# A transformer block on one Trainium2 core: twelve forget-gate sets are computed as three double blocks with the tokens standing

## The chip, the core and the metric

The kernel runs on one core of one Trainium2 chip. Its work is spread over the core's engines: TensorE multiplies matrices (PE in the profile; PEld is the loading of the operand that stands in the array), VectorE (DVE) and ScalarE (ACT) do elementwise work, GpSimd (POOL) does small work and issues DMAs, and SyncE (SP) issues DMAs alone. Each engine runs its instructions strictly in the order in which they were written for it, and waits at each one until its operands are there. The metric is the device time of one execution in microseconds (us); the kernel before takes 1574.6 us, the median of three runs.

## The reference, cut to what matters

The reference computes one block of a hybrid network on 256 tokens `x` and 256 context tokens `ctx`, all in float32. Both are normalised and modulated, and then projected by one wide matrix `w_in`, whose columns are cut into queries, keys, values, gates, forget gates and so on:

```
xn = rmsnorm(h, norm_gain[l]) * (1.0 + scale) + shift
cn = rmsnorm(hc, norm_gain[l]) * (1.0 + scale_c) + shift_c
aq, ak, av, ag, hq, hff, hfb, hi, hg, ma, mb = split_columns(xn @ w_in[l])
...
f = lbf + (1.0 - lbf) * jax.nn.sigmoid(z.astype(jnp.float32))
return to_heads(jnp.log(f)), to_heads(1.0 - f)
```

The change touches `hff` and `hfb`, the forget gates forward and backward. Each has 16 heads of 128 columns, and both are needed for the 256 tokens of `x` and the 256 of `ctx`. After the projection each value goes through a sigmoid and a scale and offset that belong to its column. The later scan over the tokens works with one column in one partition, tokens along the row. Besides the forget gates, the values `hi` and the attention's keys and values are needed for all 512 tokens too.

## The kernel before

**How a product is made.** Weights come from device memory in chunks of 128x1024 numbers by SP (`wload`, L66; five buffers, tag `raw`). ScalarE makes the high part `wh` of a chunk, VectorE the rest `wl` (`two`, L635 and L636; three buffers each). TensorE then multiplies high by high and low of the tokens, and low by high, so float32 is kept to the needed accuracy. The tokens are kept as `xHL`, high and low, with the model dimension on the partitions.

**Two ways to a product of all 512 tokens.** Both use the same scheme of seven products in place of eight, in which token halves, halves of the model dimension and column halves are combined beforehand. In each the steps 0 to 6 (`ORDER`) take weights b11, t1, t2, b22, t3, b21, t4, where the t are differences of weight chunks that VectorE makes (`combos` L616, `less` L693), and sums of tokens S stand ready in `S`.

- `quad_col(d, h0)` makes one *set*: two heads (256 columns) of the direction d, columns on the partitions. The weights stand in the array and the tokens move: per step eight matmuls of 512 columns (L660) and eight of 256 (L663, low weights by high tokens only). Its four weight loads fetch rows of 512 bytes. The results are joined by VectorE (L653, L654), go through sigmoid and scale (L682, L683), and are stored to `F_dr` by ScalarE's DMA queue.
- `quad_wide(co, dsts)` makes one *double block*: 1024 columns, tokens on the partitions. Tokens stand and weights move, so every matmul has 512 columns (L754 with high weights, L758 with low). It runs in two halves s of the model dimension; each half has seven steps of two chunks c, twelve matmuls to a chunk. Loads fetch rows of 2048 bytes. Results are taken from PSUM by ScalarE (L735, L744) and VectorE (L739) and are stored by GpSimd's queue (L726), in the second half with an adding DMA.

**Order of the work.** In this stage the order of TensorE is as written; the order on the other engines is set by a scheduler from priorities, and splits of chunks have a high one. The stage runs: three output gates, three double blocks with `quad_wide` (`hi` twice, then attention keys and values), thirteen sets with `quad_col` (of the sixteen sets, three were made at the start of the program). Then come the eight pairs of heads, which load the forget gates from `F_dr`.

**Buffers that matter here.** Tag `sm` has three tiles of 128x512 in the pool `base`. Each DMA on the two hardware queues (SP, ScalarE) takes one of eight semaphores in turn, which is seen below as DMAHW0 to DMAHW7; a DMA waits until the one that had its semaphore before has landed. DMASW are those of GpSimd's queue. `behind_chunk()` places what is issued under it behind the latest split on ScalarE and VectorE.

Of the kernel before, what the change touches and what calls it, by code (L numbers as in the profile page):

```python
# [7 lines left out]
F32 = mybir.dt.float32  # L8
F32R = mybir.dt.float32r
U8 = mybir.dt.uint8  # L10
AF = mybir.ActivationFunctionType
ALU = mybir.AluOpType
PSUM = bass.MemoryType.PSUM

P = 128
# [3 lines left out]
HD = 128  # L19
# [5 lines left out]
C_HQ, C_FF, C_FB, C_HI, C_HG = 5120, 7168, 9216, 11264, 13312  # L25
# [13 lines left out]
def block_kernel(ctx: ExitStack, tc: tile.TileContext, x, c, cx, c_ctx, w_ada, b_ada, norm_gain, w_in,  # L39
                 b_merge, lb_f, lb_b, hg_gain, w_oh, sink, w_oa, w_out, fin_gain, cst, msk, out):  # L40
    nc = tc.nc
    pe, act, dve, pool = nc.tensor, nc.scalar, nc.vector, nc.gpsimd

    def pl(name, bufs=1, **kw):
        return tc.tile_pool(name=name, bufs=bufs, **kw)
# [5 lines left out]
    base = ctx.enter_context(pl("base"))  # L51
# [3 lines left out]
    dram = ctx.enter_context(pl("dram", space=bass.MemoryType.DRAM))  # L55
# [13 lines left out]
    last_hi, last_lo = [None], [None]  # L69

    def behind_chunk():

        both = ExitStack()
        both.enter_context(tc.issue_after(last_hi[0]))
        both.enter_context(tc.issue_after(last_lo[0]))
        return both
# [103 lines left out]
    lbc = pad.tile([P, 4, 16], F32, name="lbc")  # L180
# [45 lines left out]
    few.tile([P, 16], F32, name="space1")  # L226
    gate_rows = dram.tile([KT, P], F32, name="gate_rows")
    F_dr = [[dram.tile([P, 1024], F32, name=f"F{d}_{n}") for n in range(8)] for d in range(2)]
    v_dr = [[dram.tile([P, 1024], F32, name=f"v{g}_{t}") for t in range(2)] for g in range(4)]
    hg_dr = [dram.tile([P, 1024], F32, name=f"hg{g}") for g in range(4)]  # L230
    ma_dr = [dram.tile([P, 1024], F32, name=f"ma{n}") for n in range(4)]
# [286 lines left out]
    def run(g):  # L518
        for _ in g:
            pass  # L520
# [40 lines left out]
    with pl("sp", reuse_waits="tile") as sp:  # L561
# [8 lines left out]
        def token_sums(g):  # L570

            def a(h, kh):
                return [X[:, 8 * kh + 4 * g: 8 * kh + 4 * g + 4, :].rearrange("p k (a h t) -> p k a h t", a=2, h=2)
                        [:, :, :, h, :].bitcast(F32) for X in (xH, xL)]

            def v(t):
                return t.rearrange("p (k a t) -> p k a t", k=4, a=2)

            def put(i, t):
                ks = slice(4 * g, 4 * g + 4)  # L580
                dst = [S[:, z, i, ks, :].rearrange("p k t -> p (k t)") for z in range(2)]
                act.activation(dst[0], t, AF.Copy)
                dve.tensor_tensor(dst[1], t, dst[0].bitcast(F32), op=ALU.subtract)

            def step(out, x_, y_, op):
                dve.tensor_tensor(out, x_, y_, op=op)

            a11, a12, a21, a22 = a(0, 0), a(0, 1), a(1, 0), a(1, 1)
            p, q = tmp(), tmp()
            step(v(p), a21[0], a22[0], ALU.add)  # L590
            step(v(q), a21[1], a22[1], ALU.add)
            step(p, p, q, ALU.add)
            put(0, p)
            step(v(q), v(p), a11[0], ALU.subtract)
            step(v(q), v(q), a11[1], ALU.subtract)
            put(1, q)
            for i, b in ((3, a12), (2, a22)):
                step(v(p), b[0], v(q), ALU.subtract)
                step(v(p), v(p), b[1], ALU.add)
                put(i, p)  # L600
# [30 lines left out]
        def two(src):  # L631
            h = wp.tile([P, 1024], F32R, tag="wh", name="wh", bufs=3)
            lo = wp.tile([P, 1024], F32R, tag="wl", name="wl", bufs=3)
            with tc.high_priority(PRIO):
                act.activation(h, src, AF.Copy)  # L635
                dve.tensor_tensor(lo, src, h.bitcast(F32), op=ALU.subtract)  # L636
            return h, lo

        def quad_col(d, h0):

# [43 lines left out]
                               bias=lbc[:, d, h0 + i: h0 + i + 1])  # L684
            nc.scalar.dma_start(F_dr[d][h0 // 2], F.rearrange("p i t -> p (i t)"))

        def quad_wide(co, dsts):


            def less(o, x_, y_):  # L690
                with tc.high_priority(PRIO):
                    for o_, a_, b_ in zip(o, x_, y_):
                        dve.tensor_tensor(o_, a_, b_, op=ALU.subtract)  # L693

            def weights(s):

                def load(n):
                    return [wload(w_in, 1024 * (n[0] == "2") + 512 * s + 256 * c, 2,
                                  (co + 512 * (n[1] == "2"),), 512)[0] for c in range(2)]

                u = [tmp(), tmp()]
                b11 = load("11")
                yield b11
                b12 = load("12")
                less(u, b12, b11)
                yield u
                b22 = load("22")
                less(u, b22, u)
                yield u
                yield b22  # L710
                less(b12, b22, b12)
                yield b12
                b21 = load("21")
                yield b21
                less(u, b21, u)
                yield u

            for s in range(2):
                m_ = [[bank8(), bank8()] for _ in range(3)]
                into = {0: (0, True), 1: (1, True), 2: (0, False), 3: (1, False), 4: (0, False), 5: (2, True),  # L720
                        6: (0, False)}
                kept = {}

                def store(o, t, c, z=slice(0, 2)):
                    kw = {"accum_op": ALU.add} if s else {}
                    nc.gpsimd.dma_start(dsts[c][t].rearrange("p (z c) -> p z c", z=2)[:, z, :], o, **kw)  # L726

                def done_with(i, m):

                    with tc.high_priority(2 * PRIO):  # L730
                        if i < 3:
                            kept[i] = fp.tile([P, 2, 512], F32, tag="F1" if i == 2 else "F0", name="part",
                                              bufs=1 if i == 2 else 2)
                            for z in range(2):
                                act.activation(kept[i][:, z, :], m[z], AF.Copy)  # L735
                        elif i < 6:
                            o = kept[5 - i]
                            for z in range(2):
                                dve.tensor_tensor(o[:, z, :], m[z], o[:, z, :], op=ALU.add)  # L739
                            store(o, *((0, 1), (1, 1), (0, 0))[i - 3])  # L740
                        else:
                            for z in range(2):
                                o = base.tile([P, 512], F32, tag="bb", name="part", bufs=2)
                                act.activation(o, m[z], AF.Copy)  # L744
                                store(o, 1, 0, z)

                for (i, _, st_), tiles in zip(ORDER, weights(s)):
                    z_, fresh = into[i]
                    for c in range(2):
                        h, lo = [a.rearrange("p (k c) -> p k c", k=2) for a in two(tiles[c])]  # L750
                        jz = [(j, z) for j in range(2) for z in range(2)]
                        for j, z in jz:
                            for a in range(2):
                                pe.matmul(m_[z_][z], st_(4 * s + 2 * c + j)[:, a, z, :], h[:, j, :],  # L754
                                          start=fresh and c == 0 and j == 0 and a == 0, stop=False,
                                          skip_group_check=True)
                        for j, z in jz:
                            pe.matmul(m_[z_][z], st_(4 * s + 2 * c + j)[:, 0, z, :], lo[:, j, :], start=False,  # L758
                                      stop=c == 1 and j == 1, skip_group_check=True)
                    done_with(i, m_[z_])  # L760

        with tc.manual_schedule(engines={mybir.EngineType.PE}):
            for g in range(3):
                run(output_gate(g))
                send()
                if g < 2:
                    token_sums(g)
            for co, dsts in ((C_HI, v_dr[:2]), (C_HI + 1024, v_dr[2:]), (C_K, kv_dr)):
                quad_wide(co, dsts)
            for n in range(1, 8):  # L770
                for d in range(2):
                    if (d, n) != (0, 1):
                        quad_col(d, 2 * n)

    def bias_row(row, n, late=None):
        bb = base.tile([P, 512], F32, tag="bb", name="bb", bufs=2)
# [631 lines left out]
    fg = [at.tile([P, 1024], F32, tag="v", name="fg"), None]  # L1408
# [58 lines left out]
    for i in range(4):  # L1467
        src = w_out[4 * i * P: 4 * (i + 1) * P, D - 256:].rearrange("(k p) c -> p k c", p=P)
# [7 lines left out]
    for n in range(3):  # L1476
        bo = [bank() for _ in range(2)]
        for k0 in range(0, KT, 2):
            h, lo = wchunk(w_out, k0 * P, 2, n * 512, 512)
# [8 lines left out]
    for k0 in range(0, KT, 4):  # L1488
        h, lo = wchunk(w_out, k0 * P, 4, D - 512, 256)
# [85 lines left out]
```

## Time and profile before

| what | value |
|---|---|
| runs of the kernel before | 1571.52, 1574.95, 1574.6 us; median 1574.6 us |
| profiled execution: its time, its span | 1575.11 us, 1573.3 us |
| TensorE busy | 1550.6 us of the span, 9946 matmuls |
| three double blocks | 198.36 to 426.84 us of the span |
| thirteen sets | 426.84 to 686.40 us of the span |

The profile is of one execution. A row of groups reads: line, engine, operation, output<-inputs, shape, count, then busy time, mean duration of one in ns, and the idle time of the engine just before with what ended it. A row of a stretch (windows) gives its length and, for each engine, busy us and count, then TensorE's granted clock, the share of DMA time and GB/s. A row of the timeline gives start, length, engine, line and operation, how many instructions it merges, and in brackets the idle time before it. TensorE's durations overlap (a matmul of 512 columns is shown with 389 ns, while the next begins 227 ns after it), so a pace is read from starts, not from durations.

### The profile page before, as it was taken

How to read it: one execution, taken by the hardware profiler on the slowest of the kernel's cores; microseconds unless marked ns; L12 is line 12 of the kernel's file. 1: busy time of each engine (PE TensorE's matmuls, PEld its weight loads, DVE VectorE, ACT ScalarE, POOL GpSimd, SP SyncE). 2: the span in 40 equal slices, each digit the busy share in tenths (PEclk: the TensorE clock that was granted, in tenths of full speed). 3: DMA queues.
4: the chain of work that ended last, by engine and by line, in shares of the span. 5: the costliest groups of instructions: out<-in, count | busy, mean ns of one | idle time of the engine just before them, and what ended most of it. 6: DMA issues, size and time to landing. Idle time of an engine off the chain costs nothing.

```text
span 1573.3 us, 25961 instructions
## 1 busy us (share of the span) xinstructions
PE 1550.6 (99%) x9946; PEld 1292.0 (82%) x9946; DVE 1198.4 (76%) x1758; ACT 879.5 (56%) x1380; POOL 158.4 (10%) x298
## 2 busy tenths in 40 slices
PE   7999999999999999999999999999999999999998
PEld 4558888888888888888888888888888888888887
DVE  4448987777788877879888897887977777757764
ACT  4326545454555555665566666565665767744442
POOL 2000000110100000011212221121121000000000
PEclk9999999999999999999999999999999999999999
DMA  9996645656644444477677887877777844458651
GB/s 368 386 387 237 215 156 159 180 160 183 153 121 134 135 134 134 141 266 246 235 247 239 289 276 244 282 236 242 244 256 243 281 153 157 161 186 289 226 195 68
DMA packets 232812, 339.99 MB, mean 216 GB/s; under 512 B 12368, under 2 KB 137712, under 8 KB 231920
## 3 DMA queue, kind: packets, MB, share of 16 engines
q1 hardware_dynamic: 201808, 249.54, 48.0%
q0 software_dynamic: 21376, 70.38, 14.4%
q10 hardware_dynamic: 9504, 18.42, 3.2%
q8 instruction: 78, 1.28, 0.3%
q14 instruction: 46, 0.38, 0.1%
HBM read 300.53 MB, written 37.76 MB: 215 GB/s over the span
## 4 chain that ended last, share of the span: by engine, by line
PE 89%; DMA 4%; DVE 4%; issue 2%; ACT 1%; POOL 0%; SPq 0%; POOLq 0%; DVEq 0%; ACTq 0%
PE pj L100 12%; PE pj L101 12%; PE pj L103 12%; PE pj L154 7%; PE pj L754 5%; PE pm L754 4%; PE pj L157 4%; PE pm L660 3%; PE pj L660 3%; PE pj L758 3%; DMA raw<-in_w_in_dram 2%; PE pm L758 2%; PE pa L323 2%; PE pj L427 2%; PE pj L663 2%
## 5 line engine op out<-in xcount | busy, mean ns | idle before, releaser
L85 ACT ACTIVATE wh<-raw 128x1024 fp32r<-128x1024 f32 x284 | 298.7, 1058 | 231.1 <-PE pj L101 150.6
L86 DVE TENSOR_TENSOR wl<-raw,wh 128x1024 fp32r<-128x1024 f32 x284 | 344.1, 1220 | 92.1 <-ACT wh L85 91.3
L100 PE MATMUL pj<-wh,xHL 128*128 128x512 f32 (+1 forms) x768 | 298.6, 390 | 1.1 <-ACT wh L85 1.1
L101 PE MATMUL pj<-wh,xHL 128*128 128x512 f32 (+1 forms) x768 | 294.8, 385 | 0.0
L103 PE MATMUL pj<-wl,xHL 128*128 128x512 f32 (+1 forms) x768 | 202.7, 385 | 0.0
L100 PEld LDWEIGHTS pj<-wh,xHL 128*128 128x128 f32 x768 | 144.4, 188 | 29.6 <-ACT wh L85 1.3
L101 PEld LDWEIGHTS pj<-wh,xHL 128*128 128x128 f32 x768 | 144.5, 188 | 27.6
L103 PEld LDWEIGHTS pj<-wl,xHL 128*128 128x128 f32 x768 | 142.0, 188 | 28.8
L635 ACT ACTIVATE wh<-raw 128x1024 fp32r<-128x1024 f32 x100 | 105.8, 1058 | 94.0 <-PE pj L754 37.4
L635 ACT ACTIVATE wh<-T 128x1024 fp32r<-128x1024 f32 x75 | 79.6, 1062 | 109.2 <-DVE T L616 23.4
L636 DVE TENSOR_TENSOR wl<-raw,wh 128x1024 fp32r<-128x1024 f32 x100 | 121.6, 1220 | 21.9 <-ACT wh L635 21.8
L154 PE MATMUL pj<-xHL,wh 128*128 128x512 f32 x512 | 130.3, 396 | 0.3 <-ACT wh L85 0.3
L154 PEld LDWEIGHTS pj<-xHL,wh 128*128 128x128 f32 x512 | 92.4, 189 | 17.3 <-ACT wh L85 0.5
L636 DVE TENSOR_TENSOR wl<-T,wh 128x1024 fp32r<-128x1024 f32 x75 | 91.5, 1219 | 13.6 <-ACT wh L635 13.5
L157 PEld LDWEIGHTS pj<-xHL,wl 128*128 128x128 f32 x512 | 69.8, 190 | 5.1
L204 DVE SCALAR_TENSOR_TENSOR acc<-hgw,cg,acc 128x512 f32<-128x512 f32 x60 | 44.8, 747 | 35.1 <-DMA hgw<-in_w_ada_dram 35.1
L157 PE MATMUL pj<-xHL,wl 128*128 128x256 f32 x512 | 71.3, 282 | 0.0
L928 DVE TENSOR_TENSOR A<-A,X 128x512 f32<-128x512 f32 x96 | 61.6, 683 | 0.1
L541 POOL DMA_DIRECT2D hgw<-in_w_ada_dram x64 | 35.1, 548 | 235.2 <-DVE acc L204 148.0
L754 PE MATMUL pj<-wh,S 128*128 128x512 f32 x224 | 55.3, 389 | 0.0
L660 PE MATMUL pm<-S,wh 128*128 128x512 f32 x208 | 52.5, 394 | 1.6 <-ACT s L667 1.6
L660 PE MATMUL pj<-S,wh 128*128 128x512 f32 x208 | 52.5, 394 | 0.1
(346 smaller groups left out, 2847.5 us busy)
## 6 DMA issues: line engine op xcount, KB each, us to landing
raw<-in_w_in_dram SPq DMA_DIRECT2D x300, 512.0 KB, 4.7
raw<-in_w_ada_dram SPq DMA_DIRECT2D x64, 512.0 KB, 8.0
hgw<-in_w_ada_dram POOLq DMA_DIRECT2D x64, 256.0 KB, 4.6
raw<-in_w_o_hgrn_dram SPq DMA_DIRECT2D x32, 512.0 KB, 3.7
raw<-in_w_o_attn_dram SPq DMA_DIRECT2D x32, 512.0 KB, 4.1
raw<-in_w_out_dram SPq DMA_DIRECT2D x28, 512.0 KB, 4.1
F<-F POOLq DMA_DIRECT2D x16, 512.0 KB, 6.7
F<-F ACTq DMA_DIRECT2D x13, 512.0 KB, 4.3
```

What stands on the lines that cost most here:

```text
L85: last_hi[0] = act.activation(h[:, :n], raw[:, :n], AF.Copy).ins
L86: last_lo[0] = dve.tensor_tensor(lo[:, :n], raw[:, :n], h[:, :n].bitcast(F32), op=ALU.subtract).ins
L100: pe.matmul(o, s[0], m[0], start=first, stop=False)
L101: pe.matmul(o, s[1], m[0], start=False, stop=False)
L103: pe.matmul(o, s[0], m[1], start=False, stop=last)
L154: pe.matmul(o.rearrange("p (a t) -> p a t", a=2), h[:, j, cs_], xHL[:, :, k0 + j, :T], start=k0 + j == 0, stop=False)
L157: pe.matmul(o[:, :T], lo[:, j, cs_], xH[:, k0 + j, :T], start=False, stop=k0 + j == KT - 1)
L635: act.activation(h, src, AF.Copy)
L636: dve.tensor_tensor(lo, src, h.bitcast(F32), op=ALU.subtract)
L660: pe.matmul(m_[z].rearrange("p (z a t) -> p z a t", z=2, a=2), h[:, k, :], mv(k), start=fresh and k == 0, stop=False, skip_group_check=True)
L754: pe.matmul(m_[z_][z], st_(4 * s + 2 * c + j)[:, a, z, :], h[:, j, :], start=fresh and c == 0 and j == 0 and a == 0, stop=False, skip_grou ...
L758: pe.matmul(m_[z_][z], st_(4 * s + 2 * c + j)[:, 0, z, :], lo[:, j, :], start=False, stop=c == 1 and j == 1, skip_group_check=True)
```

## The change

Of the thirteen sets twelve are no longer made by `quad_col`; the set of the backward heads 2 and 3 stays there and comes last. The 24 heads of the twelve sets (3072 columns) are made by three further calls of `quad_wide`, ahead of the other three. For that `quad_wide` takes two column starts instead of one with a fixed distance.

Since `quad_wide` leaves tokens on the partitions and the scan wants columns there, each half of 512 columns is stored to a new tensor `f_dr` of 512 tokens by 512 columns in device memory. A new generator `forget_rows` handles one head: four DMAs on SP's queue load the head's 512x128 numbers as squares of 32x32 (runs of 128 bytes) into one tile `blk`, then VectorE turns each square in one instruction into the tile `fg`, ScalarE applies sigmoid, scale and offset, and its queue stores the result to `F_dr` as before. `blk` and `fg` are both tiles of tag `sm`. `rows_on` is called ahead of a chunk's split in the double blocks (all but the first six chunks of each), and moves the head in hand one step: in the first step the DMAs, then two that do nothing, and in the next the rest, together with the first step of the following head. So a head takes three chunks. `two` now records its splits, so that `behind_chunk()` works there.

```diff
+    f_dr = [dram.tile([512, 512], F32, name=f"f{j}") for j in range(6)]
...
-                act.activation(h, src, AF.Copy)
-                dve.tensor_tensor(lo, src, h.bitcast(F32), op=ALU.subtract)
+                last_hi[0] = act.activation(h, src, AF.Copy).ins
+                last_lo[0] = dve.tensor_tensor(lo, src, h.bitcast(F32), op=ALU.subtract).ins
             return h, lo
+
+        def forget_rows(d, h, src):
+
+
+            blk = base.tile([P, 512], F32, tag="sm", name="blk", bufs=3)
+            for a in range(4):
+                part = src[:, 32 * a: 32 * a + 32].rearrange("(b r) c -> r b c", r=32)
+                nc.sync.dma_start(blk[32 * a: 32 * a + 32, :].rearrange("r (b c) -> r b c", c=32), part)
+            for _ in range(3):
+                yield
+            f = base.tile([P, 512], F32, tag="sm", name="fg", bufs=3)
+            with behind_chunk():
+                dve.transpose(f, blk)
+            act.activation(f, f, AF.Sigmoid)
+            act.activation(f, f, AF.Identity, scale=lbc[:, 2 + d, h: h + 1], bias=lbc[:, d, h: h + 1])
+            nc.scalar.dma_start(F_dr[d][h // 2][:, (h % 2) * 512: (h % 2 + 1) * 512], f)
+
+        rows_now = [iter(())]
+
+        def rows_on():
+
+            for _ in range(2):
+                try:
+                    next(rows_now[0])
+                    return
+                except StopIteration:
+                    rows_now[0] = rows_todo.pop(0) if rows_todo else iter(())
+
+        rows_todo = []
...
-        def quad_wide(co, dsts):
+        def quad_wide(cols2, dsts):
...
-                                  (co + 512 * (n[1] == "2"),), 512)[0] for c in range(2)]
+                                  (cols2[n[1] == "2"],), 512)[0] for c in range(2)]
...
-                    nc.gpsimd.dma_start(dsts[c][t].rearrange("p (z c) -> p z c", z=2)[:, z, :], o, **kw)
+                    nc.gpsimd.dma_start(dsts[c][t][:, z, :], o, **kw)
...
                     for c in range(2):
+                        if s or i > 2:
+                            rows_on()
...
+            for n, halves_ in enumerate((((0, 4), (0, 8)), ((1, 4), (1, 8)), ((0, 12), (1, 12)))):
+                two_f = f_dr[2 * n: 2 * n + 2]
+                quad_wide([(C_FF, C_FB)[d] + h * HD for d, h in halves_],
+                          [[f.rearrange("(z t p) c -> t p z c", z=2, t=2)[t] for t in range(2)] for f in two_f])
+                rows_todo.extend(forget_rows(d, h + j, f[:, j * HD: (j + 1) * HD])
+                                 for (d, h), f in zip(halves_, two_f) for j in range(4))
             for co, dsts in ((C_HI, v_dr[:2]), (C_HI + 1024, v_dr[2:]), (C_K, kv_dr)):
-                quad_wide(co, dsts)
-            for n in range(1, 8):
-                for d in range(2):
-                    if (d, n) != (0, 1):
-                        quad_col(d, 2 * n)
+                quad_wide((co, co + 512), by_rows(dsts))
+            run(rows_now[0])
+            for g in rows_todo:
+                run(g)
+            quad_col(1, 2)
```

**What moves on SP.** SP's order in the whole stage, before (-) and after (+); `raw` are weight loads (128x8x128 those of a set), `blk` the squares of one head, four DMAs each.

```order
-L66 DMA raw<-in_w_in_dram 128x2x512 x72
-L66 DMA raw<-in_w_in_dram 128x8x128 x52
+L501 DMA mkf<-in_mask_dram 128x160
+L66 DMA raw<-in_w_in_dram 128x2x512 x47
+L646 DMA blk<-f_107 32x16x32 x4
+L66 DMA raw<-in_w_in_dram 128x2x512 x2
+L646 DMA blk<-f_107 32x16x32 x4
+L66 DMA raw<-in_w_in_dram 128x2x512 x3
```

The weight loads no longer stand alone: every one to four of them four small DMAs are put in, 96 in all, beginning with the eighth load of the second double block.

**The tightest place on SP.** The second half of the second double block: `raw_2737` is its second b22 chunk, `raw_2868` and `raw_2870` are its two b21 chunks, `blk_2746` and `blk_2807` the squares of the fifth and the sixth head, whose waits on Activation are for their `sm` tiles (for these the store of an earlier `fg` must have landed too).

```order
L66 DMA raw_2737<-in_w_in_dram 128x2x512 [waits DMAHW4_49,DVE_49]
L66 DMA raw_2868<-in_w_in_dram 128x2x512 [waits DMAHW5_49,DVE_49]
L646 DMA blk_2746<-f1_108 32x16x32 [waits DMASW1_49,DMAHW6_49,DMASW0_49,Activation_49]
L646 DMA blk_2746<-f1_108 32x16x32 [waits DMAHW0_49]
L646 DMA blk_2746<-f1_108 32x16x32 [waits DMAHW1_49]
L646 DMA blk_2746<-f1_108 32x16x32 [waits DMAHW2_49]
L646 DMA blk_2807<-f1_108 32x16x32 [waits DMAHW4_49,DMAHW3_49,Activation_49]
L646 DMA blk_2807<-f1_108 32x16x32 [waits DMAHW5_49]
L646 DMA blk_2807<-f1_108 32x16x32
L646 DMA blk_2807<-f1_108 32x16x32 [waits DMAHW7_49]
L66 DMA raw_2870<-in_w_in_dram 128x2x512 [waits DMAHW0_49,DVE_49]
```

Before, the second b21 load came right after the first and waited for its buffer and its semaphore only; now eight small DMAs with waits of their own stand between.

**The same place on VectorE.** Before, the splits of b22 (`wl_2736`, `wl_2752`), the difference that takes the second b21 chunk (`T_2613`), and the splits of the next step:

```order
L636 TENSOR_TENSOR wl_2736<-raw_2694,wh_2735 128x1024 [waits PE_49,Activation_49]
L636 TENSOR_TENSOR wl_2752<-raw_2696,wh_2751 128x1024 [waits PE_49,Activation_49]
L693 TENSOR_TENSOR T_2613<-raw_2809,T_2613 128x1024 [waits DMAHW4_49,DVE_49]
L636 TENSOR_TENSOR wl_2773<-raw_2653,wh_2772 128x1024 [waits PE_49,Activation_49]
L636 TENSOR_TENSOR wl_2789<-raw_2655,wh_2788 128x1024 [waits PE_49,Activation_49]
```

and after, with the turns of the fifth and the sixth head among them:

```order
L637 TENSOR_TENSOR wl_2787<-raw_2735,wh_2786 128x1024 [waits PE_49,Activation_49]
L651 STREAM_TRANSPOSE fg_2802<-blk_2746 128x512 [waits DMAHW2_49,DMAHW7_49,DMAHW1_49,DMAHW0_49]
L637 TENSOR_TENSOR wl_2813<-raw_2737,wh_2812 128x1024 [waits PE_49,Activation_49]
L723 TENSOR_TENSOR T_2644<-raw_2870,T_2644 128x1024 [waits DMAHW0_49,DVE_49]
L637 TENSOR_TENSOR wl_2834<-raw_2694,wh_2833 128x1024 [waits PE_49,Activation_49]
L637 TENSOR_TENSOR wl_2850<-raw_2696,wh_2849 128x1024 [waits DVE_49,PE_49,Activation_49]
L651 STREAM_TRANSPOSE fg_2872<-blk_2807 128x512 [waits DMAHW6_49,DMAHW5_49,DMAHW7_49,DMAHW4_49,DVE_49]
```

VectorE now waits in its order for the squares of a head (four semaphores) as well as for weights, with the splits of the following chunks behind it.

More of the change, by code (lines that the diff above doesn't have):

```diff
@@ L767, in block_kernel, with by_rows @@
                     token_sums(g)
-            for co, dsts in ((C_HI, v_dr[:2]), (C_HI + 1024, v_dr[2:]), (C_K, kv_dr)):
-                quad_wide(co, dsts)
-            for n in range(1, 8):
-                for d in range(2):
-                    if (d, n) != (0, 1):
-                        quad_col(d, 2 * n)
+            def by_rows(a):
+                return [[t.rearrange("p (z c) -> p z c", z=2) for t in c] for c in a]
+            for n, halves_ in enumerate((((0, 4), (0, 8)), ((1, 4), (1, 8)), ((0, 12), (1, 12)))):
[4 more added lines that the diff above has]
+                                 for (d, h), f in zip(halves_, two_f) for j in range(4))
+            for co, dsts in ((C_HI, v_dr[:2]), (C_HI + 1024, v_dr[2:]), (C_K, kv_dr)):
+                quad_wide((co, co + 512), by_rows(dsts))
[3 more added lines that the diff above has]
+            quad_col(1, 2)
     def bias_row(row, n, late=None):
```

## The prediction

> **What bounds the kernel now.** I read the page first: the sums by engine, the granted clock, and the chain that ended last.
>
> ```profile
> PE 1550.6 (99%) x9946; PEld 1292.0 (82%) x9946; DVE 1198.4 (76%) x1758; ACT 879.5 (56%) x1380; POOL 158.4 (10%) x298
> PEclk9999999999999999999999999999999999999999
> PE 89%; DMA 4%; DVE 4%; issue 2%; ACT 1%; POOL 0%; SPq 0%; POOLq 0%; DVEq 0%; ACTq 0%
> ```
>
> TensorE is busy 99% of the span at full clock, and 89% of the last chain is its own. So only what shortens TensorE's stream, or the gaps in it, counts. Next the stage of the change, as stretches: the three double blocks one by one, the first set, the other twelve sets.
>
> ```profile
> 198.36:274.52 76.16, 76.16 (x337) 63.08 (x336) 60.94 (x59) 37.56 (x45) 5.33 (x8) 1.00 0.51 157
> 274.52:350.68 76.16, 76.16 (x337) 63.08 (x336) 59.39 (x56) 37.52 (x45) 7.10 (x10) 1.00 0.58 166
> 350.68:426.84 76.16, 76.16 (x337) 63.08 (x336) 59.47 (x56) 36.83 (x45) 7.10 (x10) 1.00 0.61 169
> 426.84:446.37 19.53, 19.53 (x114) 17.21 (x112) 14.62 (x17) 11.17 (x14) 1.75 (x2) 1.00 0.69 172
> 446.37:686.40 240.03, 238.25 (x1356) 208.57 (x1355) 190.23 (x215) 140.50 (x182) 5.30 (x13) 1.00 0.46 137
> ```
>
> Every double block takes 76.16 us without a gap. The first set takes 19.53 us, the other twelve 240.03 us, or 20.00 each. Why the sets are slower for the same columns is in the timeline of TensorE, by the starts: first a chunk of a double block (eight high, four low), then a step of a set (eight high, eight low of half width).
>
> ```profile
> 312.60 1.98 PE L754 MATMUL pj<-wh,xHL 128*128 128x512 f32 x8
> 314.42 1.07 PE L758 MATMUL pj<-wl,xHL 128*128 128x512 f32 x4
> 315.32 1.98 PE L754 MATMUL pj<-wh,xHL 128*128 128x512 f32 x8
> 466.39 2.00 PE L660 MATMUL pj<-xHL,wh 128*128 128x512 f32 x8
> 468.24 1.12 PE L663 MATMUL pj<-xHL,wl 128*128 128x256 f32 x8
> 469.19 2.00 PE L660 MATMUL pj<-S,wh 128*128 128x512 f32 x8
> ```
>
> A chunk takes 2.72 us, 0.227 per matmul. The step takes 1.85 us for the eight wide ones (0.231 each) and 0.95 for the eight half ones (0.119 each, not 0.113), 2.80 together. Seven steps make 19.6 us, as the first set shows. The other sets add some 0.4 us each; the waits say where:
>
> ```profile
> DVE raw L616 <- DMA raw<-in_w_in_dram: 19.5, 12, 1.9
> DVE T L616 <- DMA raw<-in_w_in_dram: 11.2, 12, 2.9
> PEld pm L660 <- ACT s L667: 2.5, 4, 0.9
> PE pm L660 <- ACT s L667: 1.6, 4, 0.7
> ```
>
> Once a set, VectorE waits for weights, ScalarE for VectorE, and TensorE for the bank that ScalarE empties.
>
> **Removed and added on TensorE.** Twelve sets go; the one that stays follows the double blocks directly, as the first set did. So 240.03 us go. Three double blocks come, 3 x 76.16 = 228.48 us: same code, same weights per block, other columns. That is **-11.55 us**, of which 12 x 19.53 - 228.48 = 5.9 is pace and 5.7 the sets' gaps. It holds if nothing new makes TensorE wait.
>
> **The cover.** How far the engines run ahead of TensorE is seen at the start of a half:
>
> ```profile
> 309.18 1.07 ACT L635 ACTIVATE wh<-raw 128x1024 fp32r<-128x1024 f32 x1 [1.66 <-PE pm L754]
> 309.90 2.35 DVE L636 TENSOR_TENSOR wl<-raw,wh 128x1024 fp32r<-128x1024 f32 x2
> ```
>
> ScalarE waits for a buffer from TensorE. Its high part, ready at 310.25, is used at 315.32: 5.1 us ahead. VectorE's first low part of the pair is ready at about 311.1 and used at 314.42: 3.3 us ahead, the least of a half. A delay below 3 us costs nothing, if VectorE can catch up.
>
> **Work added on VectorE and ScalarE.** The turn of 128x512 has no row. The nearest:
>
> ```profile
> L928 DVE TENSOR_TENSOR A<-A,X 128x512 f32<-128x512 f32 x96 | 61.6, 683 | 0.1
> L800 DVE TENSOR_TENSOR_SCAN e<-F,zero 128x255 f32<-128x255 f32 x16 | 10.1, 671 | 0.4 <-DMA F<-F 0.4
> L682 ACT ACTIVATE sg<-sg 128x512 f32<-128x512 f32 x26 | 16.0, 615 | 0.4 <-DVE sg L679 0.4
> L683 ACT ACTIVATE F<-sg,lbc 128x512 f32<-128x512 f32 x26 | 21.1, 810 | 0.5
> ```
>
> At one element a step it is 0.68 us, at the scan's pace 2 x 0.67 = 1.34. I take 0.7, since a turn carries nothing from element to element. A head takes three chunks, 8.16 us; VectorE is busy 59.4/76.16 = 78% of that already, 6.4 us, so 7.1 with the turn (7.7 at the upper bound): it fits, with 1.1 (0.5) us a head to catch up. ScalarE is at 49% and gets 0.62 + 0.81 = 1.43 us a head, 18%. Both are hidden behind TensorE; without that cover the turns would cost 24 x 0.7 = 17 us.
>
> **DMAs added.** 96 loads of squares on SP, and the stores and loads they hang on:
>
> ```profile
> raw<-in_w_in_dram SPq DMA_DIRECT2D x48, 512.0 KB, 4.2
> F<-F ACTq DMA_DIRECT2D x12, 512.0 KB, 4.3
> v<-part POOLq DMA_DIRECT2D x8, 256.0 KB, 5.8
> q1 hardware_dynamic: 16810, 24.99, 34.2%
> q1 hardware_dynamic: 51536, 27.79, 36.7%
> L66 SPq DMA_DIRECT2D raw<-in_w_in_dram x308: 367/368/1689, 18.4 to 1221.7; - x154
> ```
>
> Issue: 0.37 us, 1.5 a head. Packets: a head is 4 x 32 x 16 = 2048 runs of 128 bytes, 128 for each of 16 DMA engines. The two rows of SP's queue (the double blocks' 229 us, the sets' 260 us) give 229 x 16 x 0.342 / 16810 = 75 ns a packet of 1487 bytes on average, and 260 x 16 x 0.367 / 51536 = 30 ns at 539 bytes. A line through both gives 10 ns at 128 bytes; a price that doesn't fall below that of 539 bytes gives 30. So a head's packets take 1.3 to 3.8 us. I take 20 ns, midway, 2.6 us. With what a weight load has beside its packets (4.2 us less 16 rows of 2 KB, 16 x 0.1) some 2.6, the squares **land in 5.2 us** (3.9 to 6.4). In DMA time they add 2.6/8.16 = 32% to the 51 to 61% above: room is left. The stores of `f_dr` are as many as those of the values and as far from any reader; the last of a block land 5.8 us after issue.
>
> The squares are loaded three chunks ahead, 8.16 us, less what SP makes them wait. What bounds them is the three `sm` tiles: the squares of head h+2 need the tile of `fg` of head h, so a ring runs: turn 0.7, ScalarE 1.4, store 4.3, four issues 1.5, landing 5.2, together **13.1 us for two heads**, whose chunks take 16.3. It closes with 3.2 us to spare (2.0 to 4.5).
>
> **Loads behind squares.** SP takes its DMAs in order, so weights queue behind squares that wait for a tile. The order's tightest place is the second b21 load of a second half. Its rows before:
>
> ```profile
> 325.17 0.37 SPq L66 DMA_DIRECT2D raw<-in_w_in_dram  x1
> 319.95 1.22 DVE L636 TENSOR_TENSOR wl<-T,wh 128x1024 fp32r<-128x1024 f32 x1
> 328.67 1.23 DVE L693 TENSOR_TENSOR T<-raw,T 128x1024 f32<-128x1024 f32 x1 [0.85 <-DMA raw<-in_w_in_dram]
> 329.81 1.22 DVE L636 TENSOR_TENSOR wl<-raw,wh 128x1024 fp32r<-128x1024 f32 x1
> 336.18 1.07 PE L758 MATMUL pj<-wl,S 128*128 128x512 f32 x4
> ```
>
> After, the sixth head's squares stand ahead of it. Their tile comes free when the fourth head's row is stored: its turn follows a split like that of 319.95, so 321.2 + 0.7 + 1.4 + 4.3 = 327.6, and four issues end at 329.1. The weights go out 3.9 us late and land after 3.5 (as here) plus the squares ahead of them, 1.3 to 3.8: 333.9 to 336.4. Then the difference and the split, 2.4: 336.3 to 338.8, against 336.18 on TensorE. So 0.1 to 2.6 us there, and I take 0.7, since the squares have waited for nothing else and their packets are partly through when the load goes out. Three second halves have such a place (double blocks two, three and four): **+2.1 us**, bounds 0 and 7.8. At the other places the load has more than 5 us, or the squares wait for nothing. The first squares of a block wait for the stores of the block before, but SP has no load due then for about 10 us.
>
> **Sum.** -11.55 + 2.1 = -9.5 us on the profiled 1575.1 us (span 1573.3 and 1.8 around it): 1565.6. That execution lay 0.5 us above the median, so I predict **1565 us**.
>
> **Rivals.** (1) *Loads late in every half*: weights queue behind squares not at three places but at nearly all seven halves with squares, at the middle of the bounds, 1.4 us. Cost 9.8, time 1574.6 - 11.55 + 9.8 = 1573: no change that can be told. For it: VectorE waits for weights even now (0.85 above). Against: in most halves the load waits for its buffer, not for SP. (2) *The ring of the tiles is longer than two heads' chunks*: beyond 16.3 us every microsecond more is paid once in two heads, 12 times, since VectorE waits at the turn with all splits behind it. It decides against the kernel from a landing of 5.2 + 3.2 + 0.96 = 9.4 us, where the cost is 11.5. At 55 ns a packet, nearly twice the row of 539 bytes, squares land in 128 x 0.055 + 2.6 = 9.6 us; the ring takes 17.5, 1.2 over: +14 us, with the +2.1 above time 1579, slower. Against: both rows' packets fall with their size. (3) *Nothing waits at all*: 1574.6 - 11.55 = 1563. (4) *The change doesn't do what it says*: high matmuls of the new blocks at 0.231 instead of 0.227 would give 3 x 224 x 0.004 = 2.7 us back, 1568; against it, 28 chunks of 2.72 us make the whole 76.16, whatever stands in the array.
>
> The Trainium skill speaks for rival 2: its page "DMA: Bandwidth & Descriptors", section Specifications, says that transfers below 512 bytes are done as read-modify-write. If that doubled the time of a run, it would be the 55 ns; by that rule the sum is 1579, by the rows 1565. No row here shows a data packet under 512 bytes, so the trace can't decide, and I leave the chance at the rival's own.
>
> **How the numbers follow.** Chances: forecast 0.48 (1562 to 1569), nothing waits 0.14, slower pace 0.05, late loads 0.18, the ring 0.15. A measurement of this kernel can tell about 0.2%, 3.1 us: faster is below 1571.5, slower above 1577.7. The first three are faster, with a fifth of late loads: 0.70; the rest of late loads and a little of the ring are same, 0.17; slower 0.13. The range runs from 1560, since the runs before spread by 3.4 us, to 1577, where late loads end; above it lies the ring.
>
> **What would show it.** Right: six double blocks of 76.2 us each with TensorE gapless but for 1 us or so in the second halves of blocks two to four; squares that land in about 5 us; turns near 0.7 us. Wrong: VectorE waiting at the turn for `blk` by more than 1 us a head (the ring), or at differences for `raw` with gaps in TensorE in all halves (late loads), or a later stage that is shifted, since F of pair 1 is now the last to be stored.

## The result, and the profile after

The changed kernel takes **1587.5 us** (median of six runs, 1584.5 to 1592.4), beside 1574.3 us for the kernel before in the same comparison: a ratio of **1.009 (95% interval 1.0072 to 1.0108)**, so 0.9% slower. The forecast was 1565 us, faster, and the time lies above the range. The profiled execution has a span of 1587.5 us, 14.2 more than before.

The page of the kernel after, the sums and the last chain:

```profile
PE 1549.2 (98%) x9610; PEld 1277.1 (80%) x9610; DVE 1195.3 (75%) x1734; ACT 882.7 (56%) x1380; POOL 183.2 (12%) x328
PE 82%; DMA 9%; DVE 4%; issue 2%; SPq 2%; ACT 1%; DVEq 0%; ACTq 0%; POOLq 0%; POOL 0%
```

TensorE has 336 matmuls less, as it should, but its share of the last chain fell from 89 to 82%, and DMA's rose from 4 to 9. The six double blocks as stretches (length; busy time of PE, PEld, DVE, ACT, POOL; granted clock, DMA share, GB/s):

```profile
199.87:276.03 76.16, 76.16 (x338) 63.06 (x336) 60.82 (x59) 37.57 (x45) 6.98 (x8) 1.00 0.51 156
276.03:356.28 80.25, 77.33 (x337) 62.68 (x336) 57.06 (x58) 46.57 (x60) 7.56 (x9) 1.00 0.75 198
356.28:440.57 84.29, 78.88 (x337) 64.75 (x336) 63.16 (x63) 46.45 (x59) 8.78 (x10) 0.96 0.78 202
440.57:522.14 81.57, 78.07 (x337) 64.14 (x336) 62.66 (x63) 46.16 (x59) 7.48 (x10) 0.98 0.74 199
522.14:605.13 82.99, 78.58 (x337) 63.99 (x336) 63.33 (x63) 40.87 (x51) 7.07 (x10) 0.98 0.61 169
605.13:682.00 76.87, 76.62 (x337) 62.93 (x336) 61.54 (x60) 36.48 (x45) 7.95 (x11) 1.00 0.62 169
```

The first block has the forecast's 76.16 us to the digit. The next five, in which squares are loaded or have just been loaded, have 4.1, 8.1, 5.4, 6.8 and 0.7 us more: **25.2 us** together. With the -11.55 us of the sets that makes +13.6, nearly all of the 14.2.

Where in a block they lie is told by TensorE's timeline at the start of the third block (eight high matmuls, then four low ones):

```profile
356.28 1.99 PE L786 MATMUL pj<-wh,xHL 128*128 128x512 f32 x8
363.68 2.07 PE L790 MATMUL pj<-wl,xHL 128*128 128x512 f32 x4 [5.41 <-DVE wl L637]
365.55 3.52 PE L786 MATMUL pj<-wh,xHL 128*128 128x512 f32 x8
```

The very first chunk of the block waits 5.41 us for its low part. VectorE's timeline in the same place says for what; the kernel before follows it, in the same place of its third block, which begins at 350.68:

```profile
349.29 0.70 DVE L651 STREAM_TRANSPOSE fg<-blk 128x512 f32<-128x512 f32 x1
352.83 1.22 DVE L723 TENSOR_TENSOR T<-raw 128x1024 f32<-128x1024 f32 x1 [2.84 <-issue]
353.98 1.22 DVE L637 TENSOR_TENSOR wl<-T,wh 128x1024 fp32r<-128x1024 f32 x1
358.93 1.23 DVE L723 TENSOR_TENSOR raw<-raw 128x1024 f32<-128x1024 f32 x1 [3.74 <-DMA raw<-in_w_in_dram]
360.07 0.68 DVE L769 TENSOR_TENSOR part<-pm,part 128x512 f32<-128x512 f32 x1
360.68 1.22 DVE L723 TENSOR_TENSOR T<-raw 128x1024 f32<-128x1024 f32 x1
361.81 0.68 DVE L769 TENSOR_TENSOR part<-pm,part 128x512 f32<-128x512 f32 x1
362.41 2.35 DVE L637 TENSOR_TENSOR wl<-raw,wh 128x1024 fp32r<-128x1024 f32 x2
```

```profile
344.51 1.22 DVE L693 TENSOR_TENSOR raw<-raw 128x1024 f32<-128x1024 f32 x1
345.64 1.22 DVE L693 TENSOR_TENSOR T<-raw 128x1024 f32<-128x1024 f32 x1
346.78 1.28 DVE L739 TENSOR_TENSOR part<-pm,part 128x512 f32<-128x512 f32 x2
347.98 2.35 DVE L636 TENSOR_TENSOR wl<-raw,wh 128x1024 fp32r<-128x1024 f32 x2
```

The order is the same in both, but for one `part`. `raw<-raw` is the difference b22 - b12, computed in place. TensorE needs it only in the ninth chunk of the half (step 4, t3), some 22 us later, but nothing ties it to a place, and under high priority the scheduler puts it ahead of the splits `wl<-raw` with which the half begins. It reads the half's first b22 chunk. Before, that chunk was there. After, the load is issued 9.2 us ahead of the block's start instead of 12.0 and takes 11.8 us instead of 5.4; it lands at 358.84, and the difference starts at 358.93. (The difference b12 - b11 at 352.83 had waited too: its chunk landed at 352.75.) In the sums of VectorE's waits (total us, times, longest; stretch 274 to 684 of after, 198 to 427 of before):

```profile
DVE raw L723 <- DMA raw<-in_w_in_dram: 54.4, 18, 6.8
DVE T L723 <- DMA raw<-in_w_in_dram: 24.5, 12, 3.8
```

```profile
DVE raw L693 <- DMA raw<-in_w_in_dram: 4.6, 5, 1.4
DVE T L693 <- DMA raw<-in_w_in_dram: 6.3, 6, 1.5
```

Next comes SP, on whose queue the load stands, at the end of the second block; the third of the weight loads from 344.55 on is that first b22 chunk, at 347.07. Under it are SP's waits (274 to 684), and last the same load in the kernel before:

```profile
328.08 5.78 SPq L646 DMA_DIRECT2D blk<-f  x8
...
344.55 2.89 SPq L66 DMA_DIRECT2D raw<-in_w_in_dram  x3
347.54 8.19 SPq L646 DMA_DIRECT2D blk<-f  x3
```

```profile
SPq L646 <- DMA F<-fg: 42.6, 14, 7.5
SPq L646 <- DMA f<-part: 10.4, 1, 10.4
```

```profile
338.72 0.37 SPq L66 DMA_DIRECT2D raw<-in_w_in_dram  x1
```

SP stands at squares 14 times until an earlier row is stored, and the issues themselves are long (three in 8.19 us).

### The profile page after: what moved, and what is told of

Its sections match the earlier page's. It is cut to its first block, busy times and chain, and to the rows that moved or that the text cites. A ratio compares the mean times of both kernels' runs of the same rounds, so it can differ in the third digit from the quotient of the medians.

```text
span 1587.5 us, 25624 instructions
## 1 busy us (share of the span) xinstructions
PE 1549.2 (98%) x9610; PEld 1277.1 (80%) x9610; DVE 1195.3 (75%) x1734; ACT 882.7 (56%) x1380; POOL 183.2 (12%) x328
## 4 chain that ended last, share of the span: by engine, by line
PE 82%; DMA 9%; DVE 4%; issue 2%; SPq 2%; ACT 1%; DVEq 0%; ACTq 0%; POOLq 0%; POOL 0%
PE pj L100 12%; PE pj L101 12%; PE pj L103 12%; PE pj L154 7%; PE pj L786 6%; PE pm L786 5%; DMA raw<-in_w_in_dram 4%; PE pj L157 4%; PE pj L790 3%; PE pm L790 3%; DVE wl L637 2%; PE pj L428 2%; PE pa L324 2%; DMA qr<-qr 1%; PE al L923 1%
## 5 line engine op out<-in xcount | busy, mean ns | idle before, releaser
L786 PE MATMUL pj<-wh,S 128*128 128x512 f32 x384 | 94.9, 389 | 0.0
L786 PE MATMUL pm<-wh,S 128*128 128x512 f32 x384 | 94.9, 389 | 0.0
L786 PEld LDWEIGHTS pj<-wh,S 128*128 128x128 f32 x384 | 72.1, 188 | 15.1
L786 PEld LDWEIGHTS pm<-wh,S 128*128 128x128 f32 x384 | 72.1, 188 | 15.0
L723 DVE TENSOR_TENSOR T<-raw,T 128x1024 f32<-128x1024 f32 x48 | 58.7, 1222 | 27.2 <-DMA raw<-in_w_in_dram 26.3
L786 PE MATMUL pj<-wh,xHL 128*128 128x512 f32 x288 | 74.2, 401 | 0.0
L786 PE MATMUL pm<-wh,xHL 128*128 128x512 f32 x288 | 72.6, 395 | 0.0
```

## The experiments

At the start three theories were to be told apart. **Q**: SP stands at the squares until a tile is free, so the weights behind them are late. **P**: the small runs of the squares load the DMA engines. **D**: it is the traffic as a whole, above all the added stores to `f_dr`, half of them adding. Times are medians, ratios those to the kernel before in the same comparison; "gaps" are what the six blocks took over 6 x 76.16 us in the profiled execution.

### No squares

```diff
-            blk = base.tile([P, 512], F32, tag="sm", name="blk", bufs=3)
-            for a in range(4):
-                ... nc.sync.dma_start(blk[32 * a: 32 * a + 32, :]..., part)
-                dve.transpose(f, blk)
+                dve.transpose(f, S[:, 0, 0, 0:2, :]...)
```

> The four loads of squares per head are left out; VectorE turns a tile that always stands in the buffers (a part of S) instead, so the forget gates of the 24 heads are wrong, and everything else (double blocks, stores to device memory, turns, sigmoid, stores of F) is as in the changed kernel. Theory Q (SP stands at the squares until an earlier row has been stored, and the weights queued behind come late and in a bunch): nothing holds SP any more, the 25.2 us of gaps go, six double blocks of 76.2 us, 1587.5 - 25.2 = 1562. Theory P (the packets of 128 bytes are what loads the DMA engines): the same, 1562. Theory D (the stores to f_dr, half of them adding, fill the DMA engines at the ends of the blocks whatever SP does; squares are a small part of the bytes): gaps at the starts of blocks stay, over 12 us of them, 1575 or more.

Measured: **1565.2 us**, ratio 0.9944 (0.9923 to 0.9964), gaps 2.1 us. So the squares' loads, and what they do to others, are the loss; the stores, turns and rows of F are not, or not alone. 1.7 us of gaps stay in the third block, where the first b22 load takes 10.2 us though it is issued within 0.2 us of its time in the kernel before: that load can be late without any square.

### Turned in place

```diff
-            f = base.tile([P, 512], F32, tag="sm", name="fg", bufs=3)
+            f = blk
```

> The turn writes into the tile that it reads (fg is blk), so a head takes one of the three sm tiles instead of two, and squares wait for the store of the row three heads before, not two heads before. The same DMAs in the same order on every queue, the same bytes. Theory Q: the store waited for is one head (three chunks, 8.2 us) older; SP hardly waits for it (before: 42.6 us in 14 waits, longest 7.5), and most of the gaps go: 1562 to 1567. Theories P and D: the DMAs are the same, so the gaps stay: 1582 to 1590.

Measured: **1593.4 us**, ratio 1.0122 (1.0100 to 1.0144), gaps 25.9 us. No theory had it worse. The reason is in SP's waits of this kernel:

```profile
SPq L646 <- DMA F<-blk: 62.0, 14, 8.1
SPq L646 <- DMA f<-part: 29.3, 4, 10.2
```

They grew instead of shrinking, from 42.6 and 10.4. With one tile per head the scheduler puts squares farther ahead in SP's queue: twelve square DMAs now stand in one row at the first place, where the changed kernel has four, and wait there for the stores of `f_dr` too. So the edit moved two things at once; it says nothing against Q, and shows that the place of the squares on SP is the scheduler's.

### Squares on GpSimd's queue

```diff
-                nc.sync.dma_start(blk[32 * a: 32 * a + 32, :]..., part)
+                nc.gpsimd.dma_start(blk[32 * a: 32 * a + 32, :]..., part)
```

> The squares go out on GpSimd's queue instead of SP's, with the same tiles and waits. Theory Q: weights on SP wait for nothing but their own buffers; the squares now hold up the stores behind them on GpSimd's queue instead, which have more room: 1562 to 1570. Theories P and D: the same packets and bytes go through the same DMA engines: 1582 to 1590.

Measured: **1576.7 us**, ratio 1.0004 (0.9986 to 1.0022): some half of the loss is gone, a time between Q's forecast and that of P and D. SP waits for nothing but its weights' buffers here. The times spread widely (1569 to 1587), and the profiled execution is a long one with 18.5 us of gaps: its first b22 loads are issued up to 3.3 us later than in the kernel before and take up to 11.3 us. With SP free of the squares, the weights are still late.

### The same bytes in long rows

```diff
-            for a in range(4): ...
+            nc.sync.dma_start(blk, src)      # src: 128 whole rows of f_dr
```

> Each head's 256 KB are fetched by one DMA with 128 rows of 2048 bytes instead of four with 2048 runs of 128 bytes; the turned tile is then not the head's columns and the gates are wrong. Tiles, waits and bytes stay. Theory P: without the small runs the gaps go, 1562 to 1567. Theory Q: SP still stands until the tile's store has landed; three issues of 0.5 us per head less give back little: 1580 to 1587. Theory D: the bytes are the same, 1582 to 1590.

Measured: **1574.25 us**, ratio 0.9993 (0.9982 to 1.0005), gaps 9.5 us: again some half, which no theory had. Issues at the line of the squares, first in the changed kernel, then here, and SP's waits here:

```profile
L646 SPq DMA_DIRECT2D blk<-f x96: 302/487/6490, 287.0 to 550.3; - x96
```

```profile
L644 SPq DMA_DIRECT2D blk<-f x24: 338/339/1393, 281.4 to 534.7; - x24
```

```profile
SPq L644 <- DMA F<-fg: 53.9, 15, 8.1
```

SP waits longer for the tiles than in the changed kernel (53.9 us against 42.6), and still more than half of the gaps are gone. So the wait alone doesn't make the loss, and Q in its plain form falls. P falls in its plain form too: all of the gaps should have gone, and 9.5 us stay. What long rows took away, beside the small packets, is the time of the issues: in the changed kernel 32 issues of SP between 274 and 700 us took over 0.6 us, 46.5 us together and 6.49 at the longest; with long rows 5 did, 5.0 us together; before, none.

### The difference behind the splits

After this each half was laid out by one number: when its first b22 chunk lands, counted from the half's first matmul, against the time that its first two chunks take beyond the usual 5.44 us. The rows are of the changed kernel, from the trace, in us; blocks and halves are counted from 0, so 2.0 begins the third block. Flight is the time from issue to landing. The halves 0.1, 1.0 and 5.1, which lost nothing there, are left out.

```
half   issued   flight   landed   first two chunks too long by
1.1     -7.7      7.3     -0.5     2.7
2.0     -9.2     11.8     +2.6     8.1
2.1    -11.7      6.5     -5.1     0
3.0     -7.6      8.3     +0.6     5.4
3.1    -10.8      6.9     -3.9     0
4.0     -8.4      9.5     +1.1     5.8
4.1     -9.7      7.3     -2.4     0.8
5.0    -11.9      8.9     -3.0     0.2
(before, all but the first half: -12.0, 3.8 to 5.4, -6.6 to -8.2, 0)
```

These make 23 of the 25.2 us, and the halves that lost are those whose load landed less than 3.0 us ahead. That limit can be read from the timelines above: from the landing (358.84) to the first low matmul (363.68) VectorE needs 4.84 us for what stands in between, and the low matmuls come 1.84 us after a half's start (eight high ones at 0.23). So a new theory, **T**: one load decides, through the place of one difference. Its rival **L**: all weights are late, and the next difference would wait as long.

```diff
                 less(u, b22, u)
                 yield u
+                with behind_chunk():
+                    less(b12, b22, b12)
                 yield b22
-                less(b12, b22, b12)
                 yield b12
```

> One edit of the changed kernel: the difference b22 - b12 (L723, in place, needed by TensorE only in the ninth chunk of a half) is placed behind the splits of t2 instead of where the scheduler had put it, ahead of the splits with which a half begins. Squares, tiles, queues and stores stay. Theory T (one load decides: the first b22 chunk of a half, on which that difference stands at the head of VectorE's queue with the first splits behind it; in the changed kernel it lands up to 2.6 us after the half should begin, where 3 us ahead of it is needed): the need for it moves some 8 us later and the gaps go but for 3 us at most, 1562 to 1568. Theory L (all weights are late, and the next difference, b22 - T, would wait as long): the gaps move to later chunks, 1580 or more.

Measured: **1565.0 us**, ratio 0.9938 (0.9917 to 0.9960): faster than the kernel before. T holds; all but 2.7 us of the gaps are gone. Its third to fifth double block as stretches; then VectorE's timeline at the start of the fourth, at 428.11, and the waits of SP and of VectorE (274 to 684):

```profile
351.94:428.11 76.17, 76.17 (x338) 63.09 (x337) 63.53 (x63) 46.63 (x59) 8.74 (x10) 1.00 0.80 213
428.11:504.26 76.15, 76.15 (x337) 63.08 (x336) 60.24 (x61) 46.73 (x59) 6.25 (x9) 1.00 0.82 215
504.26:583.14 78.88, 77.12 (x338) 62.78 (x336) 63.52 (x62) 41.19 (x51) 7.93 (x11) 1.00 0.68 180
```

```profile
425.55 2.35 DVE L637 TENSOR_TENSOR wl<-raw,wh 128x1024 fp32r<-128x1024 f32 x2
428.49 1.23 DVE L637 TENSOR_TENSOR wl<-T,wh 128x1024 fp32r<-128x1024 f32 x1 [0.59 <-ACT wh L636]
429.80 1.23 DVE L723 TENSOR_TENSOR T<-raw,T 128x1024 f32<-128x1024 f32 x1
```

```profile
SPq L646 <- DMA F<-fg: 50.7, 16, 7.3
```

```profile
DVE T L723 <- DMA raw<-in_w_in_dram: 29.7, 19, 3.0
```

The splits of the half now come first, from 425.55. The first b22 chunk lands at 429.71, 1.6 us *after* the half has begun, and its first reader starts at 429.80; in the changed kernel a landing 1.1 us after cost 5.8. SP waits as long for tiles as before the edit (50.7 us), its issues are as long (37 over 0.6 us, 46.2 us together), and the DMA engines are busier (0.80 and 0.82 in the third and the fourth block, against 0.78 and 0.74). Nothing of Q, P or D was mended; what was taken away is what a late load does.

### Four chunks to a head

```diff
-            for _ in range(3):
+            for _ in range(4):
                 yield
```

> A head is moved one step per chunk as before but takes four chunks instead of three (the 24 heads then reach to the last double block), so that the row whose store is waited for is 2.7 us older at each square load, and squares load SP's queue and the DMA engines a quarter less at a time. Theory Q (the wait for the tile on SP makes the weights late): SP's waits for stores of F, 42.6 us now, fall below half, and of the 25.2 us of gaps under 10 stay: 1564 to 1573. Theory D (what slows the weights is the traffic of weights and adding stores at the ends of blocks): gaps stay above 15 us, 1577 or more.

Measured: **1587.7 us**, ratio 1.0084 (1.0058 to 1.0109), gaps 24.4 us: no gain, as D had it. SP's wait for stores of F did fall, to 22.0 us from 42.6:

```profile
SPq L646 <- DMA F<-fg: 22.0, 6, 8.4
```

That is the plainest miss of theory Q: about half the waits, the same loss. The long issues stayed (47 of them, 59.9 us together), and squares now reach into the sixth block, which loses 6.4 us.

### Stores that don't add

```diff
-                    kw = {"accum_op": ALU.add} if s else {}
+                    kw = {"accum_op": ALU.add} if s and not C_FF <= cols2[0] < C_HI else {}
```

> The stores of the second half to f_dr overwrite instead of adding, so the forget gates of the 24 heads are wrong; the number of stores and the bytes that they carry stay, but a packet of 4096 bytes is expected to take 159 ns as the plain ones do, not 328. Theory D: the double price of adding is what fills the DMA engines at the ends of blocks; the first b22 load of a half takes 6 to 7 us instead of up to 11.8, and gaps fall from 25.2 us to 12 or less: 1574 or less. Theory Q: SP's waits stay and so do most of the gaps: 1582 to 1588.

Measured: **1576.5 us**, ratio 1.0002 (0.9987 to 1.0016), gaps 12.6 us: half again, close to D's bound (12 us of gaps, 1574) and clear of Q's 1582 to 1588, though not enough to make D the cause by itself. Median landing of the larger stores to `f_dr` (274 to 684; those of both halves together), in the changed kernel and here:

```profile
f<-part POOLq DMA_DIRECT2D x13, 512.0 KB, 7.6
```

```profile
f<-part POOLq DMA_DIRECT2D x12, 512.0 KB, 5.3
```

### Both: the difference, and squares on GpSimd's queue

The diffs of the two experiments above, together.

> Both edits together: the difference behind the splits of t2, and the squares on GpSimd's queue instead of SP's. If the two effects are one (theory T: what matters is only whether the first b22 chunk is there when VectorE comes to it), there is nothing left to gain from the second: the same as with the late difference alone, 1562 to 1567. If late weights also hold TensorE elsewhere, this is 3 us or more faster than the late difference alone.

Measured: **1563.65 us**, ratio 0.9924 (0.9904 to 0.9944), the fastest of all. All six double blocks are without a gap; two of those with squares:

```profile
350.61:426.77 76.16, 76.16 (x338) 63.06 (x336) 62.81 (x63) 46.65 (x59) 26.95 (x38) 1.00 0.75 213
426.77:502.93 76.16, 76.16 (x338) 63.06 (x336) 63.42 (x64) 46.67 (x59) 25.45 (x38) 1.00 0.77 215
```

The second edit takes the 2.7 us in the fifth block that the first had left in its profiled execution, the longest of its four (1568.2 us). By the medians it is worth 1.4 us. The four times of each lie apart (1562.1 to 1564.2 here, 1564.7 to 1568.2 with the first edit alone), so the gain is likely real, but four are few. It is below the 3 us that were expected if late weights held TensorE elsewhere too.

### The difference alone, in the kernel before

The same move of the difference in the kernel before, with nothing of the change but the record of splits that `behind_chunk()` needs.

> The kernel before, with the difference b22 - b12 of its three double blocks placed behind the splits of t2, and nothing of the change. If the late difference only takes away a wait that the change brought (theory T), there is nothing to win here, since the first b22 chunk lands 6.6 to 8.2 us ahead of the half and 3 us are enough: the same time as before, 1572 to 1578, and three double blocks of 76.16 us. If the edit is worth 22 us by itself, whatever the squares do (a better order on VectorE), it shows here as about 10 us for three double blocks: 1565.

Measured: 1575.8 us, ratio 1.0003 (0.9993 to 1.0013): no change, and the three double blocks take 76.16 us each as before. The edit has no worth of its own there; it matters only where the load is late.

### Taken together

In the eight traces with VectorE's old order (the two kernels and the six experiments that leave the difference where it was), the 82 halves of double blocks other than the first half of the first block fall into two parts without an exception: in 49 the first b22 chunk landed more than 3.0 us ahead of the half, and none lost anything; in 33 it landed later, and each lost 0.2 to 8.4 us. That each of three edits (long rows, squares on GpSimd's queue, plain stores) gave back about half, 11 to 13 us, though there is only one loss of 22, fits such a limit: the lateness has several shares, and taking one away brings a good part of the halves back under it. How the lateness of one load is split among them is not settled, nor why issues on SP take so long; 32 are long in the changed kernel, at the squares and at weights near them, against 5 where runs are long and none where squares go by another queue.

## Why the prediction was wrong, step by step

- **TensorE's stream, -11.55 us: right.** Blocks of 76.16 us, and with the waits gone 1563.65 us measured against the 1563 of the rival "nothing waits". The rival of a slower pace has nothing for it.
- **The turn and its followers: right.** Priced 0.7 us with 0.62 and 0.81 on ScalarE; in the changed kernel (274 to 684):

```profile
L651 DVE STREAM_TRANSPOSE fg<-blk 128x512 f32<-128x512 f32 x24 | 16.9, 704 | 0.0
L652 ACT ACTIVATE fg<-fg 128x512 f32<-128x512 f32 x24 | 15.1, 630 | 31.5 <-DVE fg L651 30.9 <-DMA blk<-f 0.5
L653 ACT ACTIVATE fg<-fg,lbc 128x512 f32<-128x512 f32 x24 | 19.6, 816 | 0.7
```

- **The ring of the tiles: right, and rival 2 falls.** VectorE waited 0.0 us at the turn, in 24 turns. The runs of 128 bytes took 13 ns in the trace's packet records (49152 of them), below the 20 taken and far below the 55 of the rival; squares landed in 3.6 us at the median, though in 11.7 at the longest. The Trainium skill's rule on transfers below 512 bytes ("DMA: Bandwidth & Descriptors", Specifications) did not show as a doubled packet: a 512-byte packet of the sets took 27 ns, one of 128 bytes 13. A line through the packets of 512, 1024 and 2048 bytes on SP's queue (27, 46 and 84 ns) gives 13 at 128 bytes.
- **Issue of the squares: mis-sized.** 0.37 us each by the weights' row; measured 0.49 at the median and up to 6.49, 0.68 on average.
- **Loads behind squares, +2.1 us: this step failed.** The mechanism was named (weights queue behind squares that wait for a tile) and it is there: 42.6 us of SP's waits. The experiments show that these waits alone don't set the loss (53.9 us of them with long rows and 9.5 us of gaps, 22.0 with four chunks to a head and 24.4 of gaps). At the place that the prediction priced, the second b21 load of blocks two to four, TensorE lost 0.5 us in block two (VectorE waited 3.77 us there) and nothing in the others. The rest was taken at nothing, with "At the other places the load has more than 5 us, or the squares wait for nothing". There the half's first b22 load cost 23 of the 25.2 us. It had 6.6 to 8.2 us to the half's start, of which 3.0 are VectorE's: 3.6 to 5.2 to spare. The prediction set the load that it priced against the matmul that uses it. It shows no row for the first instruction of VectorE's queue that reads the b22 load, ahead of urgent splits. That row, `raw<-raw` at 344.51, stood in the trace of before, 0.40 us after the landing at 344.11. The prediction's own cover of 3 us at the start of a half is near the limit that the halves then showed, but it was not set against this load.
- **The flight of that load: mis-sized too.** It was taken as the 3.5 us of before plus packets, for loads behind squares; at the starts of the third to the sixth block it became 8 to 12 us, where weights, adding stores, squares and rows of F now meet. How much each of these adds is not shown.
- **Rival 1** ("late loads in every half") had the right kind and came next, but with 9.8 us: 1.4 for each of seven halves. Measured: six halves with 0.2 to 8.1 us each, and a few smaller gaps.

## What to carry to other kernels

The slack of a transfer is counted to the first instruction, on any in-order engine, that reads it, wherever its result is needed: work done early under high priority turns a transfer that has 20 us to spare into one that has 4. Where a change adds traffic or queue neighbours to a stage, list for each load the first reader's place in its engine's queue, and give the loads that stand ahead of urgent work their margin in numbers. And when several half-remedies each give back half, look for the one place at which lateness turns into loss, and move that.

## What the runs showed of the hardware that was not expected

**A gap costs more than its length.** After the 5.41 us gap above the next twelve matmuls start every 0.427 us instead of 0.227, for about 5 us. The changed kernel at that place, as stretches:

```profile
364.00:368.00 4.00, 4.00 (x10) 3.13 (x10) 3.97 (x4) 0.78 (x1) 1.80 (x2) 0.50 0.85 151
368.00:372.00 4.00, 4.00 (x17) 3.22 (x17) 1.73 (x3) 2.03 (x3) 0.00 (x0) 0.90 1.09 259
```

The granted clock is 0.50, ten matmuls in 4 us where 17.6 fit. Of the 25.2 us, 16.5 are idle time and 8.7 are matmuls that are longer (the busy times of the last five blocks above are that much over 5 x 76.16). The Trainium skill ("TensorE: Matmul & The Clock Gate", Part 1) puts the fall to half clock after an idle window of about 3.4 us. The 5.41 us gap agrees; but with squares on GpSimd's queue a gap of 2.04 us, the only one within 9 us, was followed, 1.5 us later, by eight matmuls at about 0.427 us, while one of 2.03 us in the same run and one of 2.40 us in the changed kernel were followed by none.

**Small runs cost most at the issue.** A packet of 128 bytes took 13 ns and one of 2048 bytes 84, so the packets of a head take each of the 16 DMA engines 1.7 us in small runs and 0.7 in long rows. But on SP's queue a DMA of 512 small runs kept SP for 0.49 us at the median and 6.49 at the longest, where a DMA of 128 rows of 2048 bytes kept it for 0.34 and 1.39: 65.6 us for the 96 DMAs of all heads, against 11.4 for the 24 with long rows. With the squares on GpSimd's queue no issue of SP took over 0.6 us.

**Adding doubles a store's packets.** A packet of 2048 bytes took 176 ns in an adding store on GpSimd's queue and 84 in a plain one on ScalarE's (the rows of F). Made plain, the second halves' stores to `f_dr` went in packets of 4096 bytes at 159 ns. The stores to `f_dr` of 512 KB, plain and adding together, land after 7.6 us at the median, and after 5.3 where all are plain (rows above).
